# Seven products of five row slices, and buffers laid out anew for each stage, in a hybrid decoder block

## The chip, the cores and the metric

The kernel runs on one core of a Trainium2 chip. The metric is the device time of one execution in microseconds, the median of three runs. A core has engines with queues of their own: TensorE (PE in the profile; PEld is its weight load), VectorE (DVE), ScalarE (ACT), GpSimd (POOL) and SyncE (SP). Here PE multiplies, ACT copies and casts, DVE adds and subtracts, SP issues nearly all loads and POOL a few adding transfers between two tiles in on-chip memory.

## The reference

One decoder block over 256 positions of width 2048, in float32: a gated feed-forward half step (FFN1), a token mixer of two head groups, and a second half step (FFN2). Cut to what the change touches:

```python
D_MODEL = 2048
SEQ = 256
D_FF = 5632

def swiglu_ffn(x, w_gate, w_up, w_down):
    return (jax.nn.silu(x @ w_gate) * (x @ w_up)) @ w_down
...
        x = x + FFN_RESIDUAL_SCALE * swiglu_ffn(rms_norm(x, ffn1_norm[l]),
                                                ffn1_w_gate[l], ffn1_w_up[l], ffn1_w_down[l])
        z = rms_norm(x, mix_norm[l]) @ w_in[l]
...
        x = x + y @ w_out[l]
        x = x + FFN_RESIDUAL_SCALE * swiglu_ffn(rms_norm(x, ffn2_norm[l]),
                                                ffn2_w_gate[l], ffn2_w_up[l], ffn2_w_down[l])
    return rms_norm(x, final_norm)
```

## The kernel before

**Tiles.** The 256 positions are two row blocks of 128 (`t`). A weight matrix is cut into units of 512 rows, four slices of 128 (`UK = 4`), and column blocks of 512 (`CW`). The model width is four units, 0 to 3; the hidden width is eleven blocks.

**A product in float32.** A number is held as a high part in a rounded format and the rest as a low part. A weight unit is loaded raw (1 MB, one SP transfer, L185); `parts_of` (L214) casts it to its high part on ACT in two halves and subtracts on DVE for the low part. `multiply` (L228) makes three matmuls for a row block and a slice: both parts of the activations by the high weights, then the high activations by the low weights.

**`seven` (L417).** For two column blocks, units 0 and 1 form a 2×2 block product with the two row blocks. It is made from seven products in place of eight, each of a sum of weight units with a sum of activation units. The sums of activations (`sf`) are made once (`seven_of`, L382; `sums`, L615). The sums of weights are made in each call: the first raw tile (w11) is overwritten three times by a DVE addition, the second (w12) gets w22 added by a POOL transfer (L464). Units 2 and 3 (`xs`) are multiplied plainly by `usual`, two column blocks each. The products run in the order p0, p4, x01, p5, x11, p6, p2, x00, p3, x10, p1 into four accumulators a, c, e, d. ACT snapshots (s1, s5, u2, u3) take a product out of an accumulator between them.

**Stages.** An FFN (L524) first makes hidden block 0 plainly, then for s = 0 to 4 a gate `seven` and an up `seven` give two hidden blocks each. After s = 0, 2 and 4 `down` (L793) multiplies the hidden blocks so far by their rows of `w_down`: column block 0, a `seven` over blocks 1 and 2, column block 3. The mixer and the output projection (`outs`) lie between the two FFNs, each with one `seven`.

**Order of the work.** Operations are issued to the engines in the order that the framework's scheduler picks, unless held (`keep_in_program_order`). SP is held to program order up to the first gate `seven` of FFN1 (`sp.held`). Each engine carries out its own queue in order, so an instruction that waits holds up all behind it. A buffer is taken up again when the last reader of what it held before is done.

**Buffers.** `raws` holds three raw tiles, `splits` two high/low pairs; every third pair comes from the FFN's own pool (`split_tiles`, L198), so three pairs turn. w11 and w12 of a call have two buffers of their own ("kept"), 13 "keep" tiles hold snapshots and sums, `bigs` ten tiles of 8 KB a partition for activations. All of them stand from the kernel's or the FFN's start to its end.

## Time and profile before

| | before |
| --- | --- |
| median of three runs | 1728.98 us (1728.04 to 1729.2) |
| profiled execution | 1726.91 us |
| its span, first to last instruction | 1725.1 us |
| instructions in the span | 20426 |
| loads from memory | 339.82 MB |

Times in a row of the profile count from the span's first instruction. In a row of a timeline stand the start, the time taken, the engine, the line, the operation, what it writes and reads, and in brackets how long the engine was idle before it and what released it. Most rows name line 43, the helper through which all engines are called, so that tiles, not lines, tell the operations apart: `hi_g_p` is the high part of a weight sum for a product of a gate call, `lo_u_x` the low part of a plain unit of an up call, `ps_d` an accumulator of a down product, `ph` a transpose of hidden values. In the row of a window the third number from the right is the granted clock of PE, as a share of full speed.

### The profile page before, as it was taken

To read this page: it belongs to the slowest core of one execution; us is meant where nothing else is said; L and a number is where in the kernel's file an instruction comes from. 1 tells how busy PE (TensorE), PEld (TensorE's weight loads), DVE (VectorE), ACT (ScalarE), POOL (GpSimd) and SP (SyncE) were. 2 spreads that over 40 slices of the span, in tenths; PEclk is the share of its full clock that TensorE was granted. 3 is DMA by queue.
4 is the path that set the end of the run, shared out by engine and by line. 5 is a ranking of instruction groups with operands and counts; after the bars stand their busy time and mean duration, and the time that the engine had idled before them with its cause. 6 is when DMAs were issued, how large, how long until landed. Compare 5 with 4: busy or idle time off the path is not lost.

```text
span 1725.1 us, 20426 instructions
## 1 busy us (share of the span) xinstructions
PE 1715.3 (99%) x7985; PEld 1432.9 (83%) x7985; DVE 1452.2 (84%) x1212; ACT 1077.8 (62%) x1406; POOL 35.3 (2%) x62
## 2 busy tenths in 40 slices
PE   9999999999999999999999999999999999999998
PEld 8888888888888888888888888888888888888886
DVE  7988889789789888787897889889788887788886
ACT  7666566656466656666965657655556664556664
POOL 0010000000000000000000000000000000000000
PEclk9999999999999999999999999999999999999999
DMA  8775777667677766655556675776777757677753
GB/s 300 225 258 174 242 234 227 214 236 233 182 238 226 227 201 219 211 160 193 175 197 205 204 251 165 228 237 224 230 227 219 244 171 243 214 225 220 254 179 128
DMA packets 178256, 372.59 MB, mean 216 GB/s; under 512 B 6132, under 2 KB 9072, under 8 KB 174448
## 3 DMA queue, kind: packets, MB, share of 16 engines
q1 hardware_dynamic: 173632, 340.81, 58.4%
q0 software_dynamic: 4352, 29.43, 8.5%
q8 instruction: 62, 1.02, 0.2%
q10 hardware_dynamic: 176, 1.06, 0.2%
q14 instruction: 34, 0.28, 0.0%
HBM read 339.82 MB, written 2.10 MB: 198 GB/s over the span
## 4 chain that ended last, share of the span: by engine, by line
PE 99%; DVE 0%; ACT 0%; DVEq 0%; issue 0%; ACTq 0%
PE ps_d L43 14%; PE ps_in L43 10%; PE ps_g_a L43 9%; PE ps_u_a L43 9%; PE ps_g_c L43 6%; PE ps_u_c L43 6%; PE ps_d_a L43 5%; PE ps_u_d L43 5%; PE ps_g_d L43 5%; PE ps_d_c L43 3%; PE ps_u_e L43 3%; PE ps_g_e L43 3%; PE ps_g L43 3%; PE ps_o L43 3%; PE ps_u L43 3%; PE ps_d_d L43 3%
## 5 line engine op out<-in xcount | busy, mean ns | idle before, releaser
L43 ACT CAST hi_g_p<-raw_g 128x1024 fp32r<-128x1024 f32 (+1 forms) x139 | 142.1, 1054 | 111.6 <-DVE raw_g L43 26.9
L43 DVE TENSOR_TENSOR lo_g_p<-raw_g,hi_g_p 128x2048 fp32r<-128x2048 f32 x70 | 159.8, 2289 | 42.3 <-ACT hi_g_p L43 41.6
L43 DVE TENSOR_TENSOR lo_u_p<-raw_u,hi_u_p 128x2048 fp32r<-128x2048 f32 x70 | 159.3, 2288 | 39.5 <-ACT hi_u_p L43 39.2
L43 ACT CAST hi_u_p<-raw_u 128x1024 fp32r<-128x1024 f32 x140 | 141.3, 1047 | 70.1 <-issue 23.1
L43 PE MATMUL ps_d<-hi_d,h 128*128 128x512 f32 x696 | 166.0, 390 | 0.0
L43 PEld LDWEIGHTS ps_d<-hi_d,h 128*128 128x128 f32 x696 | 130.0, 188 | 26.6
L43 ACT CAST hi_d<-raw_d 128x1024 fp32r<-128x1024 f32 x88 | 88.6, 1048 | 68.3 <-PE ps_u_d L43 19.9
L43 DVE TENSOR_TENSOR lo_d<-raw_d,hi_d 128x2048 fp32r<-128x2048 f32 x44 | 100.8, 2290 | 29.3 <-ACT hi_d L43 29.3
L43 PE MATMUL ps_in<-xT_nm,hi_in 128*128 128x512 f32 x512 | 122.5, 391 | 0.0
L43 ACT CAST hi_d_p<-raw_d 128x1024 fp32r<-128x1024 f32 x84 | 85.2, 1048 | 59.2 <-DVE raw_d L43 33.7
L43 PEld LDWEIGHTS ps_in<-xT_nm,hi_in 128*128 128x128 f32 x512 | 94.0, 188 | 18.8 <-ACT tha L43 0.5
L43 DVE TENSOR_TENSOR lo_d_p<-raw_d,hi_d_p 128x2048 fp32r<-128x2048 f32 x42 | 95.5, 2288 | 15.5 <-ACT hi_d_p L43 15.4
L43 ACT CAST hi_g_x<-raw_g 128x1024 fp32r<-128x1024 f32 (+1 forms) x79 | 81.2, 1058 | 42.9 <-PE ps_g_c L43 25.6
L43 ACT CAST hi_u_x<-raw_u 128x1024 fp32r<-128x1024 f32 x80 | 80.5, 1046 | 36.4 <-PE ps_u_c L43 22.1
L43 DVE TENSOR_TENSOR lo_g_x<-raw_g,hi_g_x 128x2048 fp32r<-128x2048 f32 x40 | 91.5, 2288 | 9.2 <-ACT hi_g_x L43 8.9
L43 DVE TENSOR_TENSOR lo_in<-raw_in,hi_in 128x2048 fp32r<-128x2048 f32 x32 | 73.2, 2288 | 26.7 <-ACT hi_in L43 26.3
L43 DVE TENSOR_TENSOR lo_u_x<-raw_u,hi_u_x 128x2048 fp32r<-128x2048 f32 x40 | 91.4, 2286 | 1.4 <-ACT hi_u_x L43 0.8
L43 PE MATMUL ps_d<-lo_d,h 128*128 128x512 f32 x348 | 86.2, 389 | 0.0
L43 ACT CAST hi_in<-raw_in 128x1024 fp32r<-128x1024 f32 x64 | 64.0, 1045 | 24.9 <-PE ps_in L43 15.2
L43 PEld LDWEIGHTS ps_d<-lo_d,h 128*128 128x128 f32 x348 | 65.3, 188 | 13.6
L43 DVE TENSOR_TENSOR raw_u<-raw_u,raw_u 128x2048 f32<-128x2048 f32 x30 | 68.7, 2289 | 8.5 <-DMA raw_u<-in_ffn_w_up_dram 8.1
L43 DVE TENSOR_TENSOR raw_g<-raw_g,raw_g 128x2048 f32<-128x2048 f32 x30 | 68.7, 2289 | 5.7 <-DMA raw_g<-in_ffn_w_gate_dram 5.2
(477 smaller groups left out, 3750.5 us busy)
## 6 DMA issues: line engine op xcount, KB each, us to landing
raw_d<-in_ffn_w_down_dram SPq DMA_DIRECT2D x88, 1024.0 KB, 5.2
raw_u<-in_ffn_w_up_dram SPq DMA_DIRECT2D x87, 1024.0 KB, 5.3
raw_g<-in_ffn_w_gate_dram SPq DMA_DIRECT2D x86, 1024.0 KB, 5.2
raw_in<-in_w_in_dram SPq DMA_DIRECT2D x32, 1024.0 KB, 5.1
raw_g<-raw_g POOLq DMA_DIRECT2D x10, 1024.0 KB, 7.0
raw_u<-raw_u POOLq DMA_DIRECT2D x10, 1024.0 KB, 7.0
raw_in_c<-in_w_in_dram SPq DMA_DIRECT2D x8, 1024.0 KB, 5.3
raw_o<-in_w_out_dram SPq DMA_DIRECT2D x8, 1024.0 KB, 5.2
```

The source lines that it names most:

```text
L43: ins = getattr(self.engine, name)(*args, **kwargs)
```

## The change

In the 16 gate and up calls with s = 1 to 4 (FFN1 and FFN2) the first slice of unit 2 joins unit 0, and the first slice of unit 3 joins unit 1. The seven products of these calls take five slices each, and the plain units three. A new function `fifth` makes the fifth slice's sums of activations once in each FFN, after the up call of s = 0, and writes their high and low parts into the second row block's half of `units[0]`, which `split` (L601) leaves empty. A tall raw tile takes two SP transfers (four slices and one), and POOL's addition is two transfers in place of one.

The pools `raws` and `splits` go. A stage is a pair of pools, left and right, opened by `open_stage` and freed by `close_stage`; a tile of a new stage may lie where tiles of the last one lay, and waits for the readers of those. An FFN begins with a stage of three pairs and three raw tiles. Before the gate call of s = 1 and of s = 3 it is closed and a fine stage is opened with two tall pairs, two tall, two short and two kept raw tiles; short pairs come from `bigs`. After the up call of s = 2 and of s = 4 the fine stage is closed and a stage of three pairs serves `down` and what follows. The mixer and `outs` share one stage of two pairs. The "keep" tiles go from 13 to 11, and two "spare" tiles lie in the stage.

```diff
+    def open_stage(pairs, fine=False):
+        n = stage["count"] = stage["count"] + 1
+        for side in ("left", "right"):
+            stage[side] = tc.alloc_tile_pool(name=f"stage{n}_{side}", bufs=1, side=side, reuse_waits="tile")
+        stage.update(pairs=pairs, fine=fine)
+
+    def close_stage():
+        for side in ("left", "right"):
+            stage[side].release()
+
+    def raw_tile(name, rows, kept):
+        if kept and extra:
+            pool, tag, bufs = (bigs, "big", 10) if extra[0] is bigs else (extra[0], "kept", 2)
         elif kept:
-            raw = bigs.tile([P, UK, CW], F32, tag="big", name=f"raw_{name}")
+            pool, tag, bufs = stage["right"], "kept", 2
+        elif not stage["fine"]:
+            pool, tag, bufs = stage["right"], "raw", 3
         else:
-            raw = raws.tile([P, UK, CW], F32, tag="raw", name=f"raw_{name}")
+            pool, tag, bufs = stage["right"], "tall" if rows > UK else "short", 2
+        return pool.tile([P, rows, CW], F32, tag=tag, name=f"raw_{name}", bufs=bufs)
...
+    def gather(w, cs, runs, name, kept=False):
+        raw = raw_tile(name, sum(n for _, n in runs), kept)
+        at = 0
+        for k, n in runs:
+            sp.dma_start(raw[:, at : at + n, :], w[k * P : (k + n) * P, cs].rearrange("(j p) c -> p j c", p=P))
+            at += n
+        return raw
 
-    def split_tiles(name):
-        pool, bufs = splits, 2
+    def split_tiles(name, rows=UK):
+        both = ("hi", "lo")
+        if stage["fine"] and rows < UK:
+            return [big(f"{part}_{name}")[:, :rows, :] for part in both]
+        pool, bufs = stage["left"], stage["pairs"]
         if extra:
...
     def parts_of(raw, name):
-        hi, lo = split_tiles(name)
-        for h in (slice(0, 2), slice(2, UK)):
+        rows = raw.shape[1]
+        hi, lo = split_tiles(name, rows)
+        for h in (slice(0, 2), slice(2, rows)):
             act.copy(hi[:, h, :], raw[:, h, :])
         low_part(raw, hi, lo)
...
-        nc.gpsimd.dma_start(w12, w22, accum_op=ALU.add)
+        for h in (slice(0, UK), slice(UK, w12.shape[1])):
+            if h.start < h.stop:
+                nc.gpsimd.dma_start(w12[:, h, :], w22[:, h, :], accum_op=ALU.add)
...
-                return fp.tile([P, CW], dt, tag="keep", name=name, bufs=13)
+                return fp.tile([P, CW], dt, tag="keep", name=name, bufs=11)
+
+            def spare_tile(name, dt=F32):
+                return stage["right"].tile([P, CW], dt, tag="spare", name=name, bufs=2)
+
+            open_stage(3)
...
+            xs = [of_unit(u, units[u]) for u in (2, 3)]
+            tall = [[(0, UK), (2 * UK, 1)], [(UK, UK), (3 * UK, 1)]]
+            short = [([(UK * u + 1, UK - 1)], lambda t, u=u: stationary(units[u], t)[1:]) for u in (2, 3)]
+            sf5 = {}
+
+            def fifth():
+                x = {u: f32(units[u])[:, 0] for u in (2, 3)}
+                v = keep(f"fifth{tag}")
+                exact = {u: v[:, i * S : (i + 1) * S] for i, u in enumerate((2, 3))}
+                for u, e in exact.items():
+                    dve.tensor_tensor(e, x[u][:, :S], x[u][:, S:], op=ALU.add)
+                a11, a21 = (exact[2][:, t * P : (t + 1) * P] for t in range(NT))
+                a12, a22 = (exact[3][:, t * P : (t + 1) * P] for t in range(NT))
+                w = keep(f"fifth_sums{tag}")
+                s4, s5, s6, s2 = (w[:, i * P : (i + 1) * P] for i in range(4))
+                dve.tensor_tensor(s4, a21, a22, op=ALU.subtract)
+                dve.tensor_tensor(s6, a11, a21, op=ALU.subtract)
+                dve.tensor_tensor(s5, s4, a11, op=ALU.subtract)
+                dve.tensor_tensor(s2, a12, s5, op=ALU.add)
+                home = units[0]
+                his, los = (home[:, :, o + P : o + 2 * P] for o in (0, S))
+                act.copy(his, quad(w))
+                dve.tensor_tensor(los, quad(w), f32(his), op=ALU.subtract)
+                more = {i: (his[:, q, :], los[:, q, :]) for q, i in enumerate((4, 5, 6, 2))}
+                first = {u: [stationary(units[u], t)[0] for t in range(NT)] for u in (2, 3)}
+                more.update({0: first[2][0], 1: first[3][0], 3: first[3][1]})
+                sf5.update({i: sf[i] + [more[i]] for i in sf})
...
-                seven(wg, (0, 1), cs, sf, xs, f"g{tag}_{s}", keep, gate, meanwhile, opening and s == 0)
+                if s % 2 == 1:
+                    close_stage()
+                    open_stage(2, True)
+                how = ((whole(0), whole(1)), cs, sf, xs) if s == 0 else (tall, cs, sf5, short)
+                seven(wg, *how, f"g{tag}_{s}", keep, gate, meanwhile, opening and s == 0)
                 sp.held = False
...
+                if s == 0:
+                    fifth()
+                else:
+                    if s % 2 == 0:
+                        close_stage()
+                        open_stage(3)
                 if s % 2 == 0:
                     down(s == 4)
-            extra.clear()
+            close_stage()
...
+    open_stage(2)
     with tc.tile_pool(name="mixer", bufs=1, side="left") as mp, tc.tile_pool(name="mixw", bufs=2, side="left") as mw:
```

More of the change, by code (lines that the diff above doesn't have):

```diff
@@ L179, in hybrid_block @@
     turn_of = {"split": 0}
+    stage = {"count": 0}
     def more_from(pool):
@@ L203, in split_tiles @@
                 if extra[0] is bigs:
-                    return [big(f"{part}_{name}") for part in ("hi", "lo")]
+                    return [big(f"{part}_{name}") for part in both]
                 pool, bufs = extra[0], 1
-        return [pool.tile([P, UK, CW], F32R, tag=part, name=f"{part}_{name}", bufs=bufs) for part in ("hi", "lo")]
+        return [pool.tile([P, rows, CW], F32R, tag=part, name=f"{part}_{name}", bufs=bufs) for part in both]
     def low_part(raw, hi, lo):
@@ L244, in multiply @@
                 late()
-            for j in range(UK):
-                pe.matmul(ps, st[j][0], blk[j][1], start=False, stop=end and j == UK - 1, **more)
+            for j in range(n):
+                pe.matmul(ps, st[j][0], blk[j][1], start=False, stop=end and j == n - 1, **more)
     class Norm:
@@ L412, in seven_of, with whole, of_unit @@
         return two, last, high, low
+    def whole(u):
+        return [(UK * u, UK)]
+    def of_unit(u, tile):
+        return whole(u), lambda t: stationary(tile, t)
     def quad(tile):
@@ L430, in seven, with get @@
             a, c, e, d = (bank(f"ps_{name}_{n}") for n in "aced")
[L432 to L434 removed]
+        def get(runs, n, kept=False):
+            return gather(w, slice(cols[n], cols[n] + CW), runs, f"{name}_{runs[0][0]}{n}", kept)
         (r0, r1), two = rows, len(xs) > 1
@@ L860, in down @@
                         seven(
-                            wd, (m, n), (2 * CW, CW), sh, [(u, hidden[u]) for u in us[:-2]], f"d{tag}_{m}", keep, add,
+                            wd, (whole(m), whole(n)), (2 * CW, CW), sh, [of_unit(u, hidden[u]) for u in us[:-2]],
+                            f"d{tag}_{m}", keep, add,
                             others,
@@ L973, in gate_weights @@
         def gate_weights(key, src):
-            raw = raws.tile([P, NH, P], F32, tag="raw", name=f"rawgate_{key}")
+            raw = stage["right"].tile([P, NH, P], F32, tag="raw", name=f"rawgate_{key}", bufs=3)
             nc.sync.dma_start(raw, src.rearrange("h i j -> i h j"))
@@ L1302, in hybrid_block @@
         seven(
-            w_out, (0, 1), (2 * CW, CW), so, [(u, yT[u]) for u in (2, 3)], "o_q", snapshot, done, own=own
+            w_out, (whole(0), whole(1)), (2 * CW, CW), so, [of_unit(u, yT[u]) for u in (2, 3)], "o_q", snapshot, done, own=own
         )
         extra.clear()
+    close_stage()
     fss = const.tile([P, NT, NC_D], F32, name="fss")
```

33 lines of the change are left out of this document (15 added, 18 removed).

## The prediction

> **What bounds the kernel now.** I read the cores, the page's busy times and its chain first, then the chain in order of time, then windows and timelines around the changed places.
>
> ```profile
> core 0: 1725.1 us, clock 0.999
> PE 1715.3 (99%) x7985; PEld 1432.9 (83%) x7985; DVE 1452.2 (84%) x1212; ACT 1077.8 (62%) x1406; POOL 35.3 (2%) x62
> PE 99%; DVE 0%; ACT 0%; DVEq 0%; issue 0%; ACTq 0%
> 481.15 5.44 PE ps_g_a L43 x24
> ```
>
> PE is busy for 99% of the span and the chain is PE for 99%: every matmul removed is worth its time and every stop of PE is lost whole, unless matmuls stand in it. 24 matmuls in 5.44 us are 0.2267 us each. The windows are one gate or up call each (the first two and the sum of eight, s=1 to 4 of FFN1; columns: PE, PEld, DVE, ACT, POOL, PEclk).
>
> ```profile
> 200.40:241.20 40.80, 40.80 (x182) 33.78 (x181) 31.47 (x19) 24.09 (x29) 0.85 (x1) 1.00 0.67 216
> 241.20:282.00 40.80, 40.80 (x186) 33.86 (x185) 36.33 (x22) 24.49 (x29) 0.85 (x1) 1.00 0.74 232
> sum 326.40, PE 326.40 PEld 270.74 DVE 276.11 ACT 200.29 POOL 5.16; mean PE 40.80 PEld 33.84 DVE 34.51 ACT 25.04 POOL 0.65
> ```
>
> DVE is second: 34.51 of 40.80 us, 85%. These prices serve below:
>
> ```profile
> L43 DVE TENSOR_TENSOR lo_g_p<-raw_g,hi_g_p 128x2048 fp32r<-128x2048 f32 x70 | 159.8, 2289 | 42.3 <-ACT hi_g_p L43 41.6
> L43 ACT CAST hi_g_p<-raw_g 128x1024 fp32r<-128x1024 f32 x138 | 140.2, 1048 | 111.6 <-DVE raw_g L43 26.9 <-PE ps_g_a L43 21.4 <-PE ph L43 19.0
> L43 ACT ACTIVATE u_g<-ps_g_a 128x512 f32<-128x512 f32 x20 | 11.7, 587 | 2.0 <-PE ps_g_a L43 2.0
> raw_g<-in_ffn_w_gate_dram SPq DMA_DIRECT2D x86, 1024.0 KB, 5.2
> raw_g<-in_ffn_w_gate_dram SPq DMA_DIRECT2D x4, 256.0 KB, 4.2
> 494.93 0.68 DVE L43 TENSOR_TENSOR s_g<-ps_g_d,s_g 128x512 f32<-128x512 f32 x1
> ```
>
> A DVE slice costs (2.289−0.68)/3 = 0.536 us, so five slices 2.82; ACT's second half of a tall cast, three slices, about 1.5 (two of 1.05 take 2.00).
>
> **Matmuls: −10.9 us.** A call made 15·4 = 60 slice products of three matmuls; now 7·5 + 4·6 = 59, so three fewer, 48 in the 16 calls: 48 × 0.2267 = 10.9. The call should hold 40.1 us of products.
>
> **Vector and copy work.** The splits of a call grow from 44 to 47 slices and the three sums from 12 to 15: 6 × 0.536 = 3.2 us of DVE, so 37.7 of 40.1, 94%; ACT gains three slices, 1.5 us, and stays below 70%. `fifth` (seven DVE instructions, one cast) costs under 3 us of DVE behind the s=0 work, where PE still has matmuls: nothing; uncovered it would be 3. Tall tiles take two transfers in place of one and POOL's sum two in place of one; they bring the same bytes from memory, and SP's 0.4 us an issue is short beside the call. Nothing, unless a load comes late, and there it does:
>
> **Entry to s=1 of FFN1: +12.1.** A new stage's buffers lie where the old stage's lie, so its first load waits for the old one's readers.
>
> ```profile
> 181.69 8.77 SPq L43 DMA_DIRECT2D raw_g<-in_ffn_w_gate_dram  x4
> 187.86 2.01 ACT L43 CAST hi_g_p<-raw_g 128x1024 fp32r<-128x1024 f32 x2 [1.12 <-PE ps_d L43]
> 194.71 2.00 ACT L43 CAST hi_g_p<-raw_g 128x1024 fp32r<-128x1024 f32 x2 [4.84 <-DVE raw_g L43]
> 200.35 1.98 PE L43 MATMUL ps_g_a<-hi_g_p,x 128*128 128x512 f32 x8
> ```
>
> Today the load is issued 18.7 us ahead of the first matmul, the casts of the first two products 12.5 and 5.6. In the changed program's built order the first gate load stands on SP behind a wait for the very last matmul of the down product, with all the gate loads queued behind it. PE then has nothing: landing 5.2, cast 1.05, handing over 0.3, so 6.6. It runs four matmuls (0.9) and waits for the 1.5 cast, 0.6; six more, and waits for the five-slice low part, 1.5; then the sum overwrites the raw tile (so follows that low part, 2.82) and the second product's cast stands on ACT behind the sum and the snapshot: 2.8. With 0.6 for that cast's second half: 12.1. Bounds: 6.6 if the tail is filled by a third product, 14 if the other loads come late too.
>
> **Entry to s=1 of FFN2: +6.7.** Its load waits 24 matmuls before the end, 5.44 us, so the 6.6 shrinks to 1.2 and the same tail of 5.5 follows. Bounds 1.2 and 9.
>
> **Entries to s=3: +10.0.**
>
> ```profile
> 430.23 8.53 SPq L43 DMA_DIRECT2D raw_g<-in_ffn_w_gate_dram  x3
> 439.48 2.00 ACT L43 CAST hi_g_p<-raw_g 128x1024 fp32r<-128x1024 f32 x2 [3.44 <-PE ps_d L43]
> 451.97 1.98 PE L43 MATMUL ps_g_a<-hi_g_p,x 128*128 128x512 f32 x8
> ```
>
> Here the load waits for the middle of the last down products, 10.9 us ahead, enough for 5.2. But the first cast's tile waits for the last down product's high matmuls, 8 matmuls or 1.8 us from the end, against 12.5 ahead today. The first half just makes it; the tail remains, less 0.5: 5.0 each. Bounds 0 and 7.
>
> **Inside the fine stages: +21.** Two tall pairs serve in place of three pairs, so a product's split waits for the product two before it. In s=2 and 4 the short pair has one copy.
>
> ```profile
> 575.04 1.04 ACT L43 CAST hi_u_p<-raw_u 128x1024 fp32r<-128x1024 f32 x1
> 576.17 1.98 PE L43 MATMUL ps_u_a<-hi_u_p,x 128*128 128x512 f32 x8
> 578.89 1.98 PE L43 MATMUL ps_u_c<-hi_u_p,xs 128*128 128x512 f32 x8
> 579.58 0.58 ACT L43 ACTIVATE s_u<-ps_u_a 128x512 f32<-128x512 f32 x1
> ```
>
> Today the second product's casts end at 576.08, before PE begins the first, and the snapshot of the first comes later. In the new up calls of s=2 and 4 that cast stands behind this snapshot, with no matmul between: 0.2 + 0.59 + 1.05 + 0.2 = 2.0; its low part arrives some 0.4 late; then the second snapshot, again with no matmul ahead, 0.9: some 3.4 per up. In gate calls of s=2 and 4 I count 1.3, in those of odd s 0.5 per pair: 5.2 for each of four fine stages. Bounds: 0, if the PE queue's order has slack that I take for none, and 40, if DVE sets the pace (below).
>
> **Other borders: +11.3.** Four returns to the usual stage wait for the last tall pair: 0.3 each, 1.2 (0 to 8). The mixer's first casts and FFN2's move behind other ACT work:
>
> ```profile
> 691.54 2.00 ACT L43 CAST hi_in<-raw_in 128x1024 fp32r<-128x1024 f32 x2
> 705.85 2.43 PE L43 MATMUL ps_in<-xT_nm,hi_in 128*128 128x512 f32 x10
> 705.93 0.63 ACT L43 ACTIVATE junk_nm<-xres 128x512 f32<-128x512 f32 x1 [4.44 <-DVE xres L43]
> 707.47 0.61 ACT L43 CAST xis<-xs_spare 128x512 fp32r<-128x512 f32 x1
> ...
> 1011.58 1.98 ACT L43 CAST hi_g<-raw_g 128x1024 fp32r<-128x1024 f32 x2
> 1020.26 3.79 PE L43 MATMUL ps_g<-hi_g,xT_n 128*128 128x512 f32 x16
> 1022.05 0.75 DVE L43 SCALAR_TENSOR_TENSOR xres<-s_o_q,r_y,xres 128x512 f32<-128x512 f32 x1
> 1022.90 0.63 ACT L43 ACTIVATE junk_n<-xres 128x512 f32<-128x512 f32 x1 [4.97 <-DVE xres L43]
> 1023.43 0.19 ACT L43 ACTIVATION_READ_ACCUMULATOR junk_n<-xres 128x1 f32 x1
> 1026.03 0.20 ACT L43 ACTIVATE s_n<-v_n 128x2 f32<-128x2 f32 x1
> 1034.87 0.16 DVE L43 SCALAR_TENSOR_TENSOR r_n<-q_n,y_n 128x2 f32<-128x2 f32 x1
> 1035.06 1.34 ACT L43 ACTIVATE xn<-xres,r_n 128x512 f32<-128x512 f32 x2 [2.63 <-DVE r_n L43]
> ```
>
> Today both casts are 14.3 and 8.7 us ahead of their matmuls. In the built order FFN2's first cast stands on ACT behind the whole of its norm: two adds on DVE after the last matmul (1.5), two squares with their reads (1.64), the root and seven small steps (1.4), two scalings (1.34), the cast (1.05), 0.4 for hand-overs: 7.3, with no matmul to cover it (5 to 9). At the mixer a square and the `xis` casts come before and between its halves, partly under the last matmuls: 2.8 (0 to 4).
>
> **Sum.** −10.9 + 12.1 + 6.7 + 10.0 + 21 + 1.2 + 2.8 + 7.3 = +50.2. The profiled execution took 1726.91 us (span 1725.1 and 1.8 around it), so 1777; the median is 2.1 above it: 1779.
>
> **Rivals.** The built program has 48 fewer matmuls, so that the change does what it says is not in doubt. The row is the hidden units' transposes, some 0.9 us in most calls.
>
> ```profile
> 530.86 1.03 PE L43 MATMUL ph<-ident,u_g 128*128 128x128 f32 x8
> ```
>
> - PE never stops: the old loads were that far ahead, and only the 10.9 shows: 1718. Against it: the wait on the last matmul is in the program, and 5.2 us of landing have no cover. Chance 0.04.
> - The borders alone cost (29 us): the stage inside keeps up, as DVE has 6% and PE's queue more order than I grant. 1758. For it: ACT's 61% leave room. 0.24.
> - DVE becomes the bound in the fine stages. 37.7 per call and its waits for casts, 41.6/70 × 7 = 4.2, are 41.9 against 40.1 and the transposes' 0.9: 0.9 per call, 14 in all, on top of the stops if these stop DVE as well: 1793; from three times that wait on it would pass 1800. 0.14.
> - The clock falls after a stop. Rows: every window above was granted 1.00, but the trace of before holds no stop of more than 3 us behind its start, so it can't tell. A stretch of 3 us after each of the two longest stops (6.6 and 7.3), run at half the pace, would add 3 each: 1785. 0.10. The Trainium skill has this rule ("TensorE: Matmul & The Clock Gate", What's actually happening): an idle window of some 3.4 us throttles the array to half its clock, and about as long a busy one releases it. By its figure I estimate 1.7 to 3.4 us for each stop; no run here shows it so far.
>
> The forecast itself gets 0.46, and 0.02 lies near no change, where gains and stops cancel.
>
> **How the numbers follow.** 1779 is the likeliest. Its own bounds reach 1765 to 1793; the low end goes to 1750 to hold the case of the borders alone (1758, and 8 less for FFN2's entries at their lower bounds), the high end to 1800 for DVE's. A measurement of this kernel tells 0.2%, 3.5 us, from no change. Faster by more: 0.04, the first rival; within: 0.02; slower: 0.94.
>
> **What would show it.** After the change PE has 7937 matmuls and 1704 us of busy time, and its span is some 50 longer. Idle PE of more than 6 us should stand at the first s=1 gate, released by DMA and then by the first cast, and at the start of FFN2, released by ACT; some 5 us at the first gates of the three other fine stages; 3 us in the ups of s=2 and 4, released by casts and snapshots on ACT. DVE should be near 37.7 us per call. If DVE is busy without a break where PE stops, the third rival is right; if the granted clock of a slice falls, the fourth. If the stages run in 41 us per call, the in-stage term is wrong; if PE has no stop at s=1, the reading of the waits is.

## The result and the profile after

| | before | after |
|---|---|---|
| median of 4 runs, us | 1728.51 (1726.60 to 1729.20) | 1798.76 (1795.43 to 1800.08) |
| profiled execution, us | 1726.91 | 1795.43 |
| its span, us, and granted clock | 1725.1, 0.999 | 1793.7, 0.988 |

The changed kernel takes 1.0405 times as long, 95% interval 1.0387 to 1.0424: 70 us more. The forecast was 1779 and its range 1750 to 1800. So sign and range held, the range by 1.2 us only: two of the four runs lie above 1800. And 20 us are missing from the sum; what follows is mostly about them.

The page of the changed kernel, busy times and shares of the chain that ended last:

```profile
PE 1734.6 (97%) x7937; PEld 1428.7 (80%) x7937; DVE 1500.4 (84%) x1226; ACT 1088.8 (61%) x1408; POOL 47.7 (3%) x78
PE 89%; DVE 4%; DMA 3%; ACT 2%; issue 1%; SPq 0%; DVEq 0%; POOL 0%; ACTq 0%; POOLq 0%
```

There are the 48 matmuls fewer that were foretold, yet PE is busy 19.3 us longer than before, not 11 us shorter. The chain, 99% PE before, now leaves PE for a tenth of its length. The view of PE's waits names where (what PE was to do, whom it waited for: us in total, times, longest):

```profile
PE ps_g_c L43 <- ACT hi_g_p L43: 13.6, 5, 3.3
PE ps_u_c L43 <- ACT hi_u_p L43: 9.6, 5, 2.3
PE ps_g L43 <- ACT hi_g L43: 7.6, 2, 7.0
PE ps_g_a L43 <- ACT hi_g_p L43: 7.6, 3, 6.3
PE ps_g_a L43 <- DVE lo_g_p L43: 3.6, 3, 1.2
PE ps_u_c L43 <- ACT s_u L43: 2.7, 4, 0.7
...
PE ps_d_c L43 <- DVE lo_d_p L43: 1.1, 1, 1.1
```

All of these are new, but for 0.6 us in the third row; the only stops over 0.25 us of before were 1.6 us at its very start. The first row is mostly the second product at the gates that open a fine stage, the fourth and fifth the first product there, the second and sixth the ups of s = 2 and 4, the third the start of FFN2. The last row is a low part in `down` behind a load that comes late, which the sum had not listed.

**The border to s = 1 of FFN1**, the timeline of the changed kernel (start, us, engine, what, how many; in brackets the idle time before and what ended it):

```profile
199.69 1.07 PE L43 MATMUL ps_d<-lo_d,h 128*128 128x512 f32 x4
200.79 18.38 SPq L43 DMA_DIRECT2D raw_g<-in_ffn_w_gate_dram  x10
206.00 2.42 ACT L43 CAST hi_g_p<-raw_g 128x1024 fp32r<-128x1024 f32 x2 [14.71 <-DMA raw_g<-in_ffn_w_gate_dram]
207.10 4.64 PE L43 MATMUL ps_g_a<-hi_g_p,x 128*128 128x512 f32 x10 [6.34 <-ACT hi_g_p L43]
213.97 1.55 ACT L43 CAST hi_g_x<-raw_g 128x1024 fp32r<-128x1024 f32 x2
216.52 2.07 PE L43 MATMUL ps_g_c<-hi_g_p,xs 128*128 128x512 f32 x4 [3.08 <-ACT hi_g_p L43]
```

The first load is issued as the last matmul of the down product ends (200.76), the cast starts 5.2 us later, and PE stands for 6.34. The second product's cast stands behind sum and snapshot: 3.08 more. That is the forecast's order and nearly its sizes (6.6, 2.8), with one thing besides: sum and snapshot are both over by 214.14, and the cast starts at 215.42, since the plain unit's two casts, 1.55 us, stand ahead of it on ACT as well. What is not in the forecast stands in the fourth row: ten matmuls that should take 2.3 us take 4.64.

The windows of the four calls of s = 1 and 2 of FFN1, gate and up in turn, in the columns of the prediction; ahead of them the last of the four, the up of s = 2, in the kernel before:

```profile
324.58:366.27 41.69, 41.69 (x189) 34.61 (x188) 36.43 (x23) 25.96 (x30) 0.00 (x0) 1.00 0.77 250
```

```profile
207.10:254.91 47.81, 44.73 (x178) 36.06 (x178) 41.77 (x20) 30.46 (x34) 1.74 (x2) 0.90 0.92 302
254.91:296.38 41.47, 41.47 (x186) 33.80 (x185) 38.07 (x23) 24.72 (x27) 1.75 (x2) 1.00 0.75 229
296.38:338.56 42.18, 41.99 (x186) 33.80 (x185) 38.06 (x22) 26.99 (x31) 1.76 (x2) 1.00 0.69 214
338.56:384.78 46.22, 43.25 (x186) 34.98 (x185) 36.94 (x22) 24.91 (x29) 1.75 (x2) 0.96 0.51 156
```

Before, the first of the four took 40.80 and the others, with the transposes, 41.7. (The prediction cut all its windows at 40.80, which left out up to 0.9 us of most calls.) The second and third calls stay near that; the first and last take 7.0 and 4.5 more, and these two have a granted clock below 1.00. DVE is busy 37 to 42 us in a call, 42 in the long first one; the forecast had 37.7. By the calls' true borders DVE was busy for 35.2 us in each of FFN1's eight before and is for 38.8 now: 3.6 more, where 3.2 were foretold.

**An up call of s = 2**, the timeline of the changed kernel:

```profile
328.25 2.82 DVE L43 TENSOR_TENSOR lo_g_p<-raw_g,hi_g_p 128x2560 fp32r<-128x2560 f32 x1 [2.39 <-ACT hi_g_p L43]
340.41 2.81 DVE L43 TENSOR_TENSOR raw_u<-raw_u,raw_u 128x2560 f32<-128x2560 f32 x1
342.16 0.60 ACT L43 ACTIVATE s_u<-ps_u_a 128x512 f32<-128x512 f32 x1 [1.00 <-PE ps_u_a L43]
343.31 2.42 ACT L43 CAST hi_u_p<-raw_u 128x1024 fp32r<-128x1024 f32 x2 [0.55 <-DVE raw_u L43]
344.41 1.21 PE L43 MATMUL ps_u_c<-hi_u_p,xs 128*128 128x512 f32 x4 [2.29 <-ACT hi_u_p L43]
352.48 0.73 PE L43 MATMUL ps_u_c<-hi_u_x,x 128*128 128x512 f32 x2 [0.69 <-ACT s_u L43]
```

The two stops, 2.29 and 0.69, are where they were foretold. But the cast does not wait for the snapshot ahead of it: that is over at 342.76, and the cast starts 0.55 later, when DVE's sum of five slices ends (343.22). And DVE had worked without a break since the first row, 15 us of low parts and sums, with this sum last.

**The clock.** Windows of the changed kernel around the stretches with work in which the granted clock was 0.50; three of eight, and the sum of all:

```profile
206.00:212.80 6.80, 5.70 (x13) 4.38 (x14) 4.32 (x2) 2.42 (x2) 0.00 (x0) 0.50 1.05 390
216.20:219.60 3.40, 3.08 (x7) 2.48 (x8) 2.84 (x2) 3.11 (x4) 1.12 (x2) 0.50 0.92 198
345.90:349.30 3.40, 3.40 (x9) 2.64 (x8) 3.37 (x2) 0.00 (x0) 0.00 (x0) 0.50 1.11 222
...
sum 37.60, PE 30.44 PEld 23.99 DVE 29.13 ACT 21.58 POOL 4.82; mean PE 3.80 PEld 3.00 DVE 3.64 ACT 2.70 POOL 0.60
```

Each is 3.4 or 6.8 us long. PE worked 30.44 us in them, at half the pace, so half of that, 15.2 us, is lost. The third begins 1.5 us after PE had resumed, and the stop before it was only 2.29 us. But the ups of s = 2 and 4 in FFN2 have stops of 2.32 us, at 1395.39 and 1656.07, and no such stretch follows. What tells them apart is in the trace: all eight stretches begin a whole number of 3.413 us from one another (205.97, 216.21 and 345.91, for example: 3 and 38 of them), as if the time were cut into windows of that length that do not move with the work. Two of these windows, both at full clock:

```profile
342.50:345.91 3.41, 1.50 (x6) 1.23 (x7) 0.87 (x2) 2.68 (x3) 1.75 (x2) 1.00 0.77 246
1393.81:1397.22 3.41, 1.58 (x7) 0.96 (x6) 2.72 (x1) 1.83 (x3) 0.00 (x0) 1.00 0.98 367
```

In the first PE is idle for 1.91 us, nearly the whole stop of 2.29, and half clock follows. In the second it is idle for 1.83, since the window's border cuts the stop of 2.32, and nothing follows. In this trace PE was idle for 1.91 us or more of the window just ahead of each stretch, and for at most 1.83 in every other window at full clock. In all fourteen traces no such window with less than 1.79 us idle was followed by half clock, and every one with more than 1.94 was.

**FFN2**, the timeline at its start and at its border to s = 1:

```profile
1054.33 0.63 ACT L43 ACTIVATE junk_n<-xres 128x512 f32<-128x512 f32 x1 [10.36 <-DVE xres L43]
1059.64 1.65 PE L43 MATMUL ps_g<-hi_g,xT_n 128*128 128x512 f32 x3 [6.97 <-ACT hi_g L43]
...
1250.04 24.50 SPq L43 DMA_DIRECT2D raw_g<-in_ffn_w_gate_dram  x12
1256.48 1.19 PE L43 MATMUL ps_g_a<-hi_g_p,x 128*128 128x512 f32 x4 [1.03 <-ACT hi_g_p L43]
1265.44 2.08 PE L43 MATMUL ps_g_c<-hi_g_p,xs 128*128 128x512 f32 x4 [3.30 <-ACT hi_g_p L43]
```

At the start ACT does the whole norm before the cast, with PE idle for 6.97 us. At the border the row of SP spans twelve gate loads: eight are issued within 7.3 us, three more beside POOL's two adding transfers at 1266 to 1268, one at 1274. The chain in order of time shows how long two of these transfers take:

```profile
1253.09 12.48 DMA raw_g<-in_ffn_w_gate_dram
1267.00 13.98 DMA raw_g<-raw_g
```

A load takes 12.5 us here, and POOL's two adding transfers 12.5 (1 MB) and 14.0 (256 KB), where the medians of 1 MB before were 5.2 and 7.0. Slow loads alone are not what sets this border apart: at FFN1's eight loads are issued within 6.1 us too, and take up to 11.7. But there POOL's transfers took 7.8 and 9.7, and no later product waited. Here two later products did, 1.07 and 0.91 us. The 5.5 us tail taken over from FFN1 was too short for this border.

**The account.** For each stage I took its time after less before, with the half-clock loss taken out and shown by itself (profiled executions, us):

| term | forecast | measured |
|---|---|---|
| matmuls left out | -10.9 | -10.9 |
| border to s = 1 of FFN1 | 12.1 | 10.1 |
| border to s = 1 of FFN2 | 6.7 | 9.6 |
| two borders to s = 3 | 10.0 | 11.0 |
| inside the fine stages | 21 | 21.8 |
| returns | 1.2 | 1.9 |
| mixer | 2.8 | 1.6 |
| start of FFN2 | 7.3 | 7.1 |
| a late load in the last down product | none | 1.1 |
| half clock after stops | none | 15.2 |
| sum | 50.2 | 68.5 |

A border's row is the stage before it and the gate behind it together; so the returns behind s = 2 are in the row of s = 3, and the row of the returns has the two behind s = 4. For s = 1 of FFN1 these went from 63.74 to 70.54 and from 40.80 to 47.81: 13.8; with the 0.7 of matmuls that the call no longer has 14.5; less the 4.4 lost in the first two windows at half clock above, half of 5.70 and of 3.08: 10.1. For FFN2 the same sum is 1.4 and 10.2, with the 0.7, less 2.7: 9.6.

### The profile page after: what moved, and what is told of

Read it like the earlier page. It is cut to its first block, busy times and chain, and to the rows that moved or that the text cites. A ratio compares the mean times of both kernels' runs of the same rounds, so it can differ in the third digit from the quotient of the medians.

```text
span 1793.7 us, 20426 instructions
## 1 busy us (share of the span) xinstructions
PE 1734.6 (97%) x7937; PEld 1428.7 (80%) x7937; DVE 1500.4 (84%) x1226; ACT 1088.8 (61%) x1408; POOL 47.7 (3%) x78
## 4 chain that ended last, share of the span: by engine, by line
PE 89%; DVE 4%; DMA 3%; ACT 2%; issue 1%; SPq 0%; DVEq 0%; POOL 0%; ACTq 0%; POOLq 0%
PE ps_d L43 11%; PE ps_in L43 10%; PE ps_u_a L43 9%; PE ps_g_a L43 9%; PE ps_u_c L43 6%; PE ps_g_c L43 6%; PE ps_d_a L43 5%; PE ps_u_d L43 4%; PE ps_d_c L43 3%; PE ps_g_d L43 3%; PE ps_g L43 3%; PE ps_u_e L43 2%; PE ps_o L43 2%; PE ps_d_d L43 2%; PE ps_u L43 2%; PE ps_g_e L43 2%
## 5 line engine op out<-in xcount | busy, mean ns | idle before, releaser
L43 ACT CAST hi_g_p<-raw_g 128x1024 fp32r<-128x1024 f32 (+2 forms) x139 | 164.2, 1228 | 120.1 <-DVE raw_g L43 35.9
L43 DVE TENSOR_TENSOR lo_u_p<-raw_u,hi_u_p 128x2560 fp32r<-128x2560 f32 (+1 forms) x70 | 189.0, 2713 | 50.6 <-ACT hi_u_p L43 50.6
L43 DVE TENSOR_TENSOR lo_g_p<-raw_g,hi_g_p 128x2560 fp32r<-128x2560 f32 (+1 forms) x70 | 189.4, 2714 | 46.2 <-ACT hi_g_p L43 46.1
L43 ACT CAST hi_u_p<-raw_u 128x1024 fp32r<-128x1024 f32 (+1 forms) x140 | 163.7, 1216 | 52.4 <-DVE raw_u L43 37.2
L43 DVE TENSOR_TENSOR raw_u<-raw_u,raw_u 128x2560 f32<-128x2560 f32 (+1 forms) x30 | 81.4, 2713 | 1.0 <-DMA raw_u<-in_ffn_w_up_dram 0.7
L43 DVE TENSOR_TENSOR raw_g<-raw_g,raw_g 128x2560 f32<-128x2560 f32 (+1 forms) x30 | 81.4, 2714 | 0.7 <-DMA raw_g<-in_ffn_w_gate_dram 0.2
L43 ACT CAST hi_u_x<-raw_u 128x1024 fp32r<-128x1024 f32 x80 | 67.3, 873 | 23.1 <-DMA raw_u<-in_ffn_w_up_dram 19.3
L43 DVE TENSOR_TENSOR lo_g_x<-raw_g,hi_g_x 128x1536 fp32r<-128x1536 f32 (+1 forms) x40 | 74.3, 1857 | 3.7 <-ACT hi_g_x L43 3.7
L43 DVE TENSOR_TENSOR lo_u_x<-raw_u,hi_u_x 128x1536 fp32r<-128x1536 f32 (+1 forms) x40 | 74.2, 1856 | 0.0
L43 ACT CAST hi_g_x<-raw_g 128x512 fp32r<-128x512 f32 (+2 forms) x79 | 66.6, 888 | 5.8 <-PE ps_g_c L43 2.3
```

What stands on the lines that cost most here:

```text
L43: ins = getattr(self.engine, name)(*args, **kwargs)
```

## The experiments

Twelve kernels, each in three rounds beside the kernel before, on four chips on which that one's medians were 1727.16 to 1728.59. Ratios are to it; differences between two other kernels are of their medians, not always on one chip. Theory A throughout is the forecast's account with the clock added to it; B is told with each.

### The layout without the five-slice products

```diff
-                how = ((whole(0), whole(1)), cs, sf, xs) if s == 0 else (tall, cs, sf5, short)
+                how = ((whole(0), whole(1)), cs, sf, xs) if s == 0 else ((whole(0), whole(1)), cs, sf, xs)
```

Stages and two pairs stay, all blocks have four slices as before.

> The changed kernel's stages, pools and two pairs, but every product and plain unit of the fine calls takes four slices as before (7985 matmuls; DVE and ACT work as before). Theory A (the loss is that of the layout): the border stops stay, 6.3 and some 2 at the first gate in FFN1, 6 in FFN2, 3.5 twice at s=3, 7 at the start of FFN2, 1.6 at the mixer, 1 at the returns, with 9 of slow clock; inside the stages little, since DVE has more air: 40 more than before, 1768, 1758 to 1780. Theory B (the five-slice work is the cause): 1740 or less.

Measured: 1780.0 us (1777.31 to 1781.53), ratio 1.0299, 1.0283 to 1.0314. That is the very end of theory A's range. So the layout alone costs 52.8 us of the 70; the five-slice products add the other 17 or so instead of taking 10.9 away. Windows of this kernel, the gate and up of s = 1 and the up of s = 2 in FFN1:

```profile
207.62:254.54 46.92, 44.35 (x181) 35.73 (x182) 41.80 (x21) 30.80 (x35) 1.71 (x2) 0.93 0.94 321
254.54:296.26 41.72, 41.72 (x190) 34.62 (x189) 33.10 (x23) 22.69 (x28) 0.85 (x1) 1.00 0.66 205
338.02:380.26 42.24, 41.87 (x190) 34.43 (x188) 31.23 (x22) 22.90 (x29) 0.00 (x0) 1.00 0.55 170
```

The border is as dear as in the changed kernel (46.92 against 47.81); the call inside a stage costs what it did before, 41.7, and the even up 0.5 more, against 4.5 in the changed kernel. So the borders' stops come from where the buffers lie, and the even ups' stops from five-slice work on two pairs: with four slices, cast and sum are shorter and mostly hidden.

### Matmuls that nobody reads in the stops

```diff
+    def warm(ps, tile, n):
+        pe.held = True
+        for _ in range(n):
+            pe.matmul(ps, tile[:, 0, :P], tile[:, 0, :], start=True, stop=True, skip_group_check=True)
+        pe.held = False
...
+            if i in (0, 4) and name in WARM:
+                warm(ps, xs[0][2], WARM[name][i // 4])
```

143 matmuls more (the 149 of the expectation are a wrong sum of its own numbers), ahead of the first and second products where PE stops and at the start of FFN2; what they write is overwritten by the product behind them. Waits and buffers are as in the changed kernel.

> The changed kernel with work added: matmuls whose result is overwritten are put into the stops (26 and 12 at the first gate of s=1 in FFN1, 4 and 13 in FFN2, 12 ahead of the second product at s=3, 9 in the ups of s=2 and 4, 28 at the start of FFN2; 0.2267 us each, sized to end before the awaited cast). Theory A (the granted clock falls because PE stands still, and the matmuls after a stop run at half pace for up to 3.4 us windows, 15 us in all): the slow windows go and the kernel gets faster by 10 to 15 with 149 matmuls more: 1786, 1783 to 1790. Theory B (the slow matmuls behind the stops have another cause, such as loads that come late): 1798 or more.

Measured: 1782.06 us (1779.17 to 1783.27), ratio 1.0307, 1.0291 to 1.0322: 16.7 us less than the changed kernel, with more matmuls; a little more than theory A gave. The profiled execution's span is 1779.4 us and its clock 0.998. The timeline at the border to s = 1 of FFN1:

```profile
201.35 6.05 PE L44 MATMUL ps_g_a<-x 128*128 128x512 f32 x26
206.90 2.42 ACT L44 CAST hi_g_p<-raw_g 128x1024 fp32r<-128x1024 f32 x2 [14.96 <-DMA raw_g<-in_ffn_w_gate_dram]
208.00 1.20 PE L44 MATMUL ps_g_a<-hi_g_p,x 128*128 128x512 f32 x4 [0.59 <-ACT hi_g_p L44]
```

The load is as late as ever and the real matmuls begin at the same place; they only run at full pace, and no stretch with work in it is granted 0.50. This settles that the clock term is real, caused by the stops, and near the size read from the windows: 15.2 in the profiled execution, whose clock was 0.988 (the two profiled spans differ by 14.3); the changed kernel's other runs had 0.984 to 0.986, and so lost more.

The Trainium skill says of this ("TensorE: Matmul & The Clock Gate", What's actually happening) that an idle window of about 3.4 us throttles the array to half its clock. The lengths of 3.4 and 6.8 us and the 0.50 agree. That the array must be idle for a whole window doesn't: 1.91 us of 3.41 were enough above.

### A pool for each pair and each kind of tile

```diff
-        for side in ("left", "right"):
-            stage[side] = tc.alloc_tile_pool(name=f"stage{n}_{side}", bufs=1, side=side, reuse_waits="tile")
...
+        stage["right"] = {tag: pool(tag, "right") for tag in tags}
+        stage["left"] = [pool(f"pair{k}", "left") for k in range(pairs)]
+        stage.update(pairs=pairs, fine=fine, turn=FIRST_PAIR.get(n, 0))
...
+        pool = stage["left"][stage["turn"] % stage["pairs"]]
+        stage["turn"] += 1
```

The first tiles of a fine stage now lie where tiles of the last stage lay that are done with early, so their loads and casts need not wait for the last down product.

> The changed kernel with each tag of a stage in a pool of its own, so that the fine stage's kept raw tiles lie exactly on the old kept and spare tiles (free since the down call's seven products, 16 us or more ahead), and with the pairs taken in a fixed turn, chosen so that the first tall pair lies on pairs that come free before the last unit. Same computation, same transfers. Theory A (the stops at the stage borders come from where the buffers lie): the 6.34 us stop at the first gate of s=1 in FFN1 and the late loads at that of FFN2 go, with some 4 us of slow clock behind them; the second product's cast still waits there, 2 to 3 us at each of four borders; the ups of s=2 and 4, whose casts now stand ahead of the snapshot in the built order, lose their 3.0 us each and two slow windows of 1.7. 9 + 5 + 2.4 + 15.4 = 32 less: 1767, 1755 to 1775. Theory B (five-slice casts, sums and low parts are what is late): less than 5 gained, 1793 or more.

Measured: 1812.37 us (1810.74 to 1814.24), ratio 1.0485, 1.0469 to 1.05: 14 us slower than the changed kernel, far outside theory A. It lies in B's open range, but not for B's cause. The borders were cured as A had it: the last down block and the first gate of FFN1's s = 1 take 63.93 and 43.56 us (changed kernel: 70.54, 47.81), those of FFN2 63.89 and 43.48 (65.16, 51.02). But a stop of up to 4.6 us came fourteen times inside the calls, 43 us in all. The timeline of this kernel:

```profile
257.66 1.04 ACT L44 CAST hi_u_p<-raw_u 128x1024 fp32r<-128x1024 f32 x1 [6.70 <-DMA raw_u<-raw_u]
261.25 1.22 PE L44 MATMUL ps_u_c<-hi_u_x,x 128*128 128x512 f32 x2 [4.62 <-ACT s_u L44]
```

PE waits for the snapshot `s_u`, which waits for nothing but its turn: ahead of it on ACT stands the cast of product 6, and that waits 6.70 us for POOL's adding transfer. With the buffer free earlier, the cast of product 6 had moved ahead in ACT's order.

Two kernels put it back, by an edge that orders it behind the casts of product 5 and adds no semaphore: the first for the first half of that cast, the second for both.

```diff
+        fifth_cast = act.last
...
+        act.behind = fifth_cast if len(r0) > 1 else None
```

```diff
+        act.behind, act.times = (fifth_cast, 2) if len(r0) > 1 else (None, 1)
```

> The kernel of the first experiment with one thing more: in the fine calls the cast for p6, which waits for POOL's adding transfer, is pinned on ACT behind the cast for p5, so that it can't hold up the snapshot s5. Theory A (14 stops of 1.4 to 4.6 us there, 43 in all, come from that cast at the head of ACT's queue): these go with some 10 of slow clock, while two ups get a stop ahead of p4 of 2 to 2.5: 1762, 1755 to 1768. Theory B (the five-slice work on DVE is what is late, and the stop only moves): 1795 or more.

> The placed kernel with both halves of the cast for p6 pinned behind the cast for p5; the run before last but two pinned the first half alone, and the second half went on ahead of the snapshot s5 and waited there for POOL's transfer. Theory A (that wait at the head of ACT's queue makes the 14 stops of 2.4 to 5.6 us ahead of the plain unit x01, 60 in all): they go with their slow clock, and some of it comes back as shorter waits for DVE ahead of p5: 1798, 1785 to 1808. Theory B (DVE is late there whatever ACT does): 1845 or more.

Measured: 1854.8 us (1852.24 to 1857.9), ratio 1.0734, with one half (1762 had been expected), and 1775.62 us (1775.28 to 1778.02), ratio 1.0279, 1.0264 to 1.0295, with both. With one half, the other now went ahead alone and waited longer; the timeline of the kernel with one half:

```profile
260.10 1.47 ACT L44 CAST hi_u_p<-raw_u 128x1536 fp32r<-128x1536 f32 x1 [8.41 <-DMA raw_u<-raw_u]
262.12 2.93 PE L44 MATMUL ps_u_c<-hi_u_x,x 128*128 128x512 f32 x6 [5.56 <-ACT s_u L44]
```

With both, the snapshot waits for nothing but its product, and the fourteen stops are gone; the time is below the 1785 to 1808 that were expected. One cast's place in one queue is worth 37 us (1812 to 1776) or, half done, costs 42. And the placement with that place restored is 23 us faster than the changed kernel. In the profiled executions the two borders to s = 1 make 20 of them, half clock included (118.35 to 107.20 us and 116.18 to 107.14, the stage before and the gate together): for these the borders' reading holds.

### FFN2's first cast ahead of its norm

```diff
-                (0, "g"): [flush],
+                (0, "g"): [flush_behind if tag == 2 else flush],
```

`flush_behind` keeps on ACT the norm's work behind what was issued before it, the first casts.

> The changed kernel with one thing done: in FFN2 the squares and transposes of the norm that are still owed are pinned on ACT behind the casts of the first gate unit. Theory A (that cast is late only because it stands behind the norm's chain on ACT): the 6.97 us stop at the start of FFN2 goes, and 1.5 us of slow clock behind it: 1790, 1787 to 1793. Theory B (the cast waits for its buffer, the pair of the last output product): 2 us gained at most, 1797 or more.

Measured: 1788.39 us (1787.26 to 1790.09), ratio 1.0344, 1.0326 to 1.0361; 10.4 us less in the medians, as expected, and 5.4 in the profiled spans (1793.7 and 1788.3). At the place itself, from the first output product to FFN2's first gate `seven`, it is 4.8 (141.66 to 136.83 us, 1.5 of it half clock), so that the expected time came partly by luck. The timeline:

```profile
1052.53 3.79 PE L43 MATMUL ps_g<-hi_g,xT_n 128*128 128x512 f32 x16
1057.73 2.11 PE L43 MATMUL ps_g<-lo_g,xT_n 128*128 128x512 f32 x8 [1.41 <-DVE lo_g L43]
```

The stop of 6.97 us is gone; the norm, now behind the cast, delays the low part instead, 1.41 us, and a later use of the norm, 1.9. The same pin together with the filled stops (and without fillers at FFN2's start):

> The changed kernel with FFN2's owed squares behind its first cast and the stops filled (none at FFN2's start, where no stop is left). The two cures together: the filled kernel's 1782 less the 7.0 us stop of FFN2: 1775, 1772 to 1778. If the stop comes back elsewhere: 1780 or more.

Measured: 1777.68 us (1775.96 to 1779.14), ratio 1.0288, 1.0272 to 1.0303. On top of the filled stops, where no half clock is left to save, the pin gains 4.4.

With the placement and one half of product 6's cast put back:

> The kernel of the run before with FFN2's owed squares pinned behind its first cast as in the second experiment. The two cures lie at different places and add up: 10 less than the run before, 1752, 1745 to 1758. If the time lost there is only handed to another wait: within 3 of the run before.

Measured: 1850.06 us (1848.9 to 1856.66), ratio 1.0714: 4.7 less than without the pin, but a hundred off, since the kernel it was built on had the fourteen stops. There the first gate cast waited for its own load, 4.15 us: SP had later tiles' loads ahead of it.

### The second product's cast against the snapshot

```diff
+            act.held = len(rows[0]) > 1
             s1 = snap(a, "s1")
+            act.held = False
```

The snapshot is kept behind the cast of the second product.

> The changed kernel with one thing done: in the 16 fine calls the snapshot of the first product is pinned on ACT behind the casts of the second. Theory A (the stop ahead of the second product is ACT's order): in four ups 2.3 us each go, two of them with 1.7 of slow clock, and some 0.8 at three borders: 14 less, 1785, 1780 to 1790. Theory B (the cast waits for the sum of weights on DVE, which is late as DVE is full): 3 at most, 1796 or more.

Measured: 1801.62 us (1796.08 to 1802.32), ratio 1.0415, 1.0398 to 1.0432: no gain, as theory B had it. At three borders the stop ahead of the second product did shrink (3.08 to 1.90, and twice to 2.5); in the ups it did not. The timeline of the same up call:

```profile
343.59 2.81 DVE L43 TENSOR_TENSOR raw_u<-raw_u,raw_u 128x2560 f32<-128x2560 f32 x1
346.52 2.42 ACT L43 CAST hi_u_p<-raw_u 128x1024 fp32r<-128x1024 f32 x2 [2.17 <-DVE raw_u L43]
347.61 1.95 PE L43 MATMUL ps_u_c<-hi_u_p,xs 128*128 128x512 f32 x4 [2.35 <-ACT hi_u_p L43]
```

The cast stands first now and still waits for DVE's sum; PE stops for 2.35. The next kernel put that sum ahead of a low part on DVE as well, on the base with one half put back:

> The kernel of the run before with the low part of the first plain unit pinned on DVE behind the first sum of weights, and the first snapshot on ACT behind the casts for p4. Theory A (the cast for p4 waits for a sum that stands behind that low part on DVE): the stops ahead of p4 at the four borders and in two ups, 1.6 to 2.6 each, go with their slow clock: 15 less, 1737, 1730 to 1745. Theory B (DVE has no time left there whatever the order): 5 at most.

Measured: 1867.11 us (1866.52 to 1868.2), ratio 1.0803: 17 us slower than its base. On that base it says little of the theory; the stops at the second product of the gates grew, from 9.1 to 11.7 us in all, and those behind the snapshot from 60.3 to 73.6. Those at the second product of the ups went, from 3.2 to 0.2. Whether the sum alone can be brought ahead at a gain in the whole stays open.

### Less work for DVE

```diff
-        dve.tensor_tensor(lo, raw, f32(hi), op=ALU.subtract)
+        engine = nc.gpsimd if hi.shape[1] == UK - 1 else dve
+        engine.tensor_tensor(lo, raw, f32(hi), op=ALU.subtract)
```

The low parts of the three-slice units go to POOL, on the placed kernel with both halves, FFN2's pin and FFN2's loads in program order.

> The placed kernel with p6's cast behind p5's, FFN2's squares behind its first cast, FFN2's loads in program order up to the first gate, and the low parts of the three-slice plain units (four a call, 1.75 us each) on POOL in place of DVE. Theory A (the stops left inside the stages are DVE's share of the five-slice work: 37.7 us a call and its waits): with 7.0 us a call off DVE the calls come near 42 us and the whole to 1745, 1735 to 1770, if POOL takes up to 3.5 us for such a part; no row shows what it takes, and from 5 on it is late itself: 1800. Theory B (two pairs and the order on ACT make them): 1780 or more with POOL under 3.5.

Measured: 1854.63 us (1852.16 to 1862.92), ratio 1.0747. The groups by line:

```profile
L44 DVE TENSOR_TENSOR lo_u_p<-raw_u,hi_u_p 128x2560 fp32r<-128x2560 f32 x56 | 207.5, 3726 | 55.6 <-ACT hi_u_p L44 55.6
L258 POOL TENSOR_TENSOR lo_u_x<-raw_u,hi_u_x 128x1536 fp32r<-128x1536 f32 x32 | 156.8, 4905 | 186.5 <-ACT hi_u_x L44 162.1 <-PE ps_u_c L44 24.5
```

4.9 us each, where DVE takes 1.75. But the slow low parts are the smaller loss: PE waits 7.6 us for low parts of POOL's, and 34.2 at the second product for DVE's. For DVE slowed down too: 100 of its 160 five-slice low parts and sums ran beside a subtraction of POOL's and took 4.18 us in the mean, up to 6.15; the 60 others took 2.82, as in the changed kernel. With 112 us of subtractions taken off it, DVE was busy for 1544.4 us, 44 more than there. So the run did not relieve DVE and can't tell whether DVE's load holds the calls back.

### All the cures together

Placement with other first pairs, both halves put back, FFN2's pin, the loads of FFN2 kept in their order on SP, and the snapshot behind the cast:

```diff
+FIRST_PAIR = {3: 2, 4: 0, 5: 2, 6: 1, 9: 2, 10: 0, 11: 2}
...
+            sp.held = True
```

> All cures that worked, in one kernel: the buffers placed and the pairs' turn chosen for all four borders, both halves of p6's cast behind p5's, FFN2's squares behind its first cast and its loads in program order up to the first gate, the first snapshot behind the casts for p4. From the run with both halves (1776): less 8.9 at FFN2's start (a stop of 7.0 and its slow clock), less 3 at s=3: 1764, 1759 to 1770. That stays above the kernel before, because what is left lies inside the stages (two tall pairs with five-slice work) and at the returns. If it is under 1740, the borders and orders were the whole loss; if it is 1775 or more, the stop at FFN2 comes back as another wait.

Measured: 1761.72 us (1760.09 to 1764.5), ratio 1.0195, 1.0178 to 1.0212. It is the fastest of the kernels with five-slice products, 37 us under the changed one, and still 34 above the kernel before; the time lies in the range expected. The windows of the four calls of s = 1 and 2 of FFN1:

```profile
202.59:245.52 42.93, 41.23 (x179) 32.65 (x177) 39.29 (x20) 29.10 (x33) 1.74 (x2) 1.00 0.80 252
245.52:286.64 41.12, 41.12 (x187) 33.97 (x185) 37.36 (x23) 24.90 (x28) 1.76 (x2) 1.00 0.77 234
286.64:329.57 42.93, 42.40 (x186) 33.73 (x185) 40.50 (x23) 27.28 (x31) 1.76 (x2) 1.00 0.75 237
329.57:376.39 46.82, 42.64 (x187) 33.58 (x185) 36.36 (x23) 24.77 (x29) 1.75 (x2) 1.00 0.45 134
```

All at full clock, 173.8 us against 165.9 before. The odd up, 41.12, has what the forecast granted a call with nothing in its way (40.1 of products and the transposes). The last window holds 2.75 us for a late first load of the down product. What remains in the gates, 2.1 us over before at s = 1 and 1.2 at s = 2, was not taken apart: two pairs, the five-slice splits and late transfers are all still in it. At s = 2 two pairs alone don't make it: in the layout with four slices that gate took 41.76 us, as before.

## Why the prediction was right, and where it was short

- **Bound and matmuls.** PE was the bound; 7937 matmuls came. The forecast 1704 us of busy time did not: 1734.6. Of the 30.6 between them 15.2 are the half clock. The other 15 are time in which PE counts as busy without more matmuls, such as the first group behind a stop (four in 1.20 us at full clock in the run with the stops filled, where 0.91 is their price); the stage times hold it, the waits don't. It was not taken apart further.
- **Entry to s = 1 of FFN1.** Right: the load behind the last matmul, the first stop (6.34 for 6.6), the tail. Placing the tiles elsewhere took it away (70.54 and 47.81 to 63.93 and 43.56), and four-slice work in the same layout did not. The sum had the plain unit's casts ahead of the second product's at nothing; it came out 2 us too high all the same.
- **Entry to s = 1 of FFN2.** Mis-sized: 9.6 for 6.7, and above its bound of 9. The prediction put the same tail of 5.5 behind a first stop of 1.2. The first stop came (1.03), and the second product's (3.30); what it missed are POOL's adding transfers of up to 14.0 us, issued beside three more loads, which make later products late too. That these transfers slow each other is argued from the trace; no run spread them out.
- **Entries to s = 3 and returns.** 11.0 for 10.0 and 1.9 for 1.2: right within 2 us together.
- **Inside the fine stages.** 21.8 for 21, but the size was better than its reason. The step had the second product's cast "behind this snapshot"; the run with the snapshot put behind the cast shows that the cast of the ups waits for DVE's sum, and nothing is gained there by the order on ACT. The sum is late because DVE had 15 us of work in a row ahead of it. That five slices and not the two pairs alone cause it is shown by the layout with four slices, where the even up takes 42.24 for 46.22.
- **Mixer and FFN2's start.** 1.6 for 2.8 and 7.1 for 7.3. With the cast put first, the stop at FFN2 went.
- **The clock, the step that failed.** The prediction had this as a rival with a chance of 0.10, "a stretch of 3 us after each of the two longest stops", 6 us, and left it out of the sum. It is no other way in which the change could go: it comes on top of the forecast's stops wherever these come. And it came eight times, since 1.91 us of idle time in a window of 3.41 were enough: at every one of the four borders, at FFN2's start and in two of the four even ups, the other two having escaped by where the window's border fell. The two longest stops made only 4.4 of it. In all it was 15.2 us, five sixths of the 18.3 that the sum was short in the profiled execution. With the stops filled it is gone, and the time, 1782, is 3 above the forecast's. The range had its upper end at 1800 for DVE as the bound; that the clock's loss fitted under it is luck.
- **The other rivals.** PE did stop, and the stages inside did not keep up, so the first two fell. For DVE as the bound: by the prediction's own sign, DVE busy without a break where PE stops, this rival is right in the even ups, where the sum that PE waits for ends 15 us of unbroken work. It is not right for the calls as a whole: in the up of s = 2 DVE stands idle for 9 us behind that stop, 6.0 of them waiting for casts, and at the borders it waits for the casts too. It is a link of the chain in places (4% of it), not the pace. The run meant to relieve it slowed it instead, so for what is left in the gates it stays open.

## What to carry to other kernels

A stop of the matrix engine can cost more than its length: put that into the sum itself. In the changed kernel it was 1.5 to 2.9 us more. All stops of 3 us and more had a stretch at half clock behind them there, those of 2.3 us in two cases of four, as the window's border fell. Where a stop cannot be removed, fill it with matmuls into a bank that is overwritten. When buffers are laid out anew, look for the first load and the first cast behind each border and ask which reader frees their place, and how far that reader is from the end. Then read every in-order queue again: an instruction that became free to go early can take the head of the queue and wait there for a transfer, with work behind it that is due sooner. And before work is handed to another engine, see whether the two slow each other.

## What the runs showed of the hardware

- In the changed kernel the granted clock fell to 0.50 in stretches of 3.4 or 6.8 us, once 1.5 us after work had resumed and behind a stop of 2.29 us. The stretches lie on a fixed grid of 3.413 us. In the fourteen traces half clock followed a window of that grid at full clock when PE was idle for more than 1.94 us of it, and never when it was idle for less than 1.79. 143 matmuls more made the program 16.7 us faster.
- POOL's subtraction of 128x1536 took 4.8 to 4.9 us in the mean (3.5 to 6.1), DVE's 1.75. A DVE operation on two tiles of 128x2560 took 2.82 us alone and 4.18 in the mean, up to 6.15, beside such a subtraction.
- An adding transfer of 1 MB by POOL took 7.0 us (median before). Issued beside three loads, one of 1 MB took 12.5 and one of 256 KB 14.0.
